# A hybrid decoder trunk on one core: the last half norm on two columns, wider output strips, and other DMA constants in the list scheduler

## The chip, the cores and the metric

The kernel runs on one NeuronCore of one Trainium2 chip. The metric is the device time in microseconds (us) of one execution. Three runs of the kernel before took 1483.68, 1481.92 and 1483.88 us; their median is 1483.68 us. With three runs spread over 2 us, differences of about 0.2% (3 us) can be told from none.

## What is computed

Two decoder layers over 512 tokens of width 1024, all in float32. Layer 0 mixes tokens with multi-scale retention, layer 1 with an mLSTM; each is followed by a convolutional feed-forward block. Every block is entered through an RMS norm with shift, scale and gate from a conditioning vector, and a last RMS norm ends the trunk:

```python
for i in range(2):
    h = rmsnorm(x, norm_tok_g[i]) * (1 + sc_t) + sh_t
    x = x + gt_t * (retention_mixer(h) if i == 0 else mlstm_mixer(h))
    h = rmsnorm(x, norm_ffn_g[i]) * (1 + sc_f) + sh_f
    x = x + gt_f * conv_ffn(h)
return rmsnorm(x, final_g)     # x * rsqrt(mean(x*x, -1) + 1e-6) * final_g
```

## The kernel before, in words

**Layout.** The residual stream lies transposed in SBUF: eight tiles `x[0]` to `x[7]` of 128 channels by 512 tokens (KT = 8). Every float32 product is made of three products of rounded parts (`mm3`, L654): a high part (`hi`, written by a copy on ACT into float32r) and a low part (`lo`, the rest). The low part of a weight comes either from one subtraction on DVE (`low_part`, L500) or from a negated copy on ACT followed by a DMA that accumulates the raw weight onto it, issued by GpSimd (`low_part_added`, L505). Weights are loaded by plain DMAs on SyncE's queue (SP), 512 KB each. Many projections are done with a seven-product block scheme (`Fold`, L547), whose sums of weight blocks are made on DVE (tiles `ws`, `wt`).

**Buffers.** Weights and all that is made from them share 18 wide slots (tag `w`: `raw`, `wa`, `wb`, `whi`, `wlo`, `ws`, `wt`, `wv`, `out`), and activations share 62 slots (tag `s`). Two more slots (tag `a`) serve the loads of the conditioning weights (`ada`) and of the down projection inside the feed-forward loop (`Beside`, L527).

**Who sets the order.** The program is first recorded as a list of calls, then a list scheduler orders it (`Plan`, L149), and each engine executes its calls in that order. For each call it has a modelled duration. `order` (L218) gives each call a due time: TensorE's calls follow one another without gaps, and every other call is due early enough for the calls that need it, less its own duration and a tail. `tail` (L261) is a short latency for engine work; for a plain DMA it is its transfer time plus 3.0 us, for an accumulating one plus 4.5 us. `run` (L264) then simulates the engines. A plain DMA of 512 KB takes 0.4 us of SP's time, then waits until 1.2 us have gone by and the modelled DMA is free, moves for 1.33 us, and counts as landed 1.2 us later (L357; 2.4 us for an accumulating one). Among the ready calls of an engine, the one with the earliest due time goes first. A call that opens a new buffer may start only if its buffer ranks, by due time, within the free slots of its kind (`makers`, L293), and not over 35 us ahead of its due time (EARLY). The scheduler's times exist only to choose an order; on the chip, semaphores hold each call until its data is there.

**The feed-forward loop.** `Ffn.items` (L1435) runs units 4 to 21 of the 22 pairs of up-projection tiles as 18 repeated units of one seven-product scheme each, in both layers (`folded`, L867), with the down projection of earlier groups inside (`downs`, L1439).

**The end.** The last group of the down projection is done in two halves of 256 tokens (`boundary`, L1067; HALVES, L59): eight `po` products for the first half, then eight for the second. After each product DVE adds it to `x[m]` (`add_residual`, L1031), ACT squares the half (`SquareSum.add`, L679) and DVE adds the squares up. In the second half the last two tiles' squares are not added but multiplied in directly (`direct = (0, 2)`, L1217). The root of the mean of squares (`SquareSum.root`, L694) is a product with a 128 by 128 matrix of 1/1024, so all 128 partitions hold the mean of each of the 256 tokens; then ACT takes a square root and DVE a reciprocal, both over 128 by 256 elements. `End.use` (L1222) multiplies each tile by its gain and the root in one DVE instruction and sends the output: the first half in two DMAs of four tiles while the second half is computed, the second half at the very end in four DMAs of two tiles (`End.rest`, L1240).

The same norm is already done on columns at the start of the program (`means`, L1602, and L1656 to L1666): there the tokens lie on partitions, four columns of 128, and are turned back by a product with a unit matrix. Its rows in the trace serve the prediction.

Of the kernel before, what the change touches and what calls it, by code (L numbers as in the profile page):

```python
# [10 lines left out]
F32 = mybir.dt.float32  # L11
F32R = mybir.dt.float32r
I32 = mybir.dt.int32
AF = mybir.ActivationFunctionType
ALU = mybir.AluOpType

P = 128
T = 512
D = 1024
KT = D // P  # L20
# [6 lines left out]
GROUPS = [4, 4, 4, 4, 6]  # L27
# [5 lines left out]
VADDED = (1, 6, 5, 7, 3)  # L33
SWAPPED = (64, 67, 75, 150, 153, 158, 188, 192, 200, 208, 209, 211, 222, 241, 287, 301, 313)
FOLD_FROM = 4
WPAD = 64
OFF = 16
DIRECT = (0, 0)
# [21 lines left out]
HA, HB = slice(0, 256), slice(256, 512)  # L60
# [88 lines left out]
class Plan:  # L149
# [109 lines left out]
        return self.run()  # L259

    def tail(self, c):  # L261
        return c.lat if not c.dma else c.dma + (4.5 if "accum_op" in c.k else 3.0)

    def run(self):  # L264
        calls = self.calls
# [3 lines left out]
        pe_at, lag, dma_free, table, issued = 0, 0.0, 0.0, None, set()  # L269
# [55 lines left out]
        while len(out) < len(calls):  # L325
            if not any(best.values()):
                held = [(calls[n].eng, calls[n].name, [b.args[4] for b in calls[n].bufs])
                        for e in engines for _, n in wait[e][:4]]
                live = [(b.args[4], b.uses) for b in {id(b): b for c in calls for b in c.bufs}.values()
                        if b.bufs and b.log is None and b.uses]  # L330
                print(len(live), live)
                raise RuntimeError(f"{len(out)} of {len(calls)}: {[b.args[4] for b in calls[pe[pe_at]].bufs]} {held}")
            t, e, n = min(c for c in best.values() if c)
            c, dirty = calls[n], {e}
            for b in c.bufs:
                if b.log is not None:
                    b.log, b.busy = None, 0.0
                    if b.bufs:
                        b.at = room[b.key].pop(0)[1]
                        dirty.update(engines)  # L340
                        makers[b.key].remove(b.maker)
            occ = c.occ
            if e == "POOL" and c.shared:
                port = (t, t + occ)
            elif e == "DVE" and c.shared:
                occ += SHARE * max(0.0, min(t + occ, port[1]) - max(t, port[0]))
            if c.fn and c.fn != table:
                table, occ = c.fn, occ + 1.3
            wait[e].remove((c.due, n))
            if e == "PE":  # L350
                issued.add(n)
                while pe_at < len(pe) and pe[pe_at] in issued:
                    pe_at, lag = pe_at + 1, t - calls[pe[pe_at]].due
            free[e] = t + occ
            if c.dma:
                dma_free = max(dma_free, t + occ + 1.2) + c.dma
                c.end = dma_free + (2.4 if "accum_op" in c.k else 1.2)  # L357
            else:
                c.end = t + occ + c.lat
            for b in c.bufs:  # L360
                b.busy = max(b.busy, c.end)
                b.uses -= 1
                if not b.uses and b.bufs:
                    insort(room[b.key], (b.busy, b.at))
                    dirty.update(engines)
            for m, real in c.succs:
                s = calls[m]
                s.left -= 1
                s.ready = max(s.ready, c.end if real else t + occ)
                if not s.left:  # L370
                    dirty.add(s.eng)
                    insort(wait[s.eng], (s.due, m))
            out.append(n)
            self.log.append((t, n, occ))
            for d in dirty:
                best[d] = choose(d)
# [10 lines left out]
def trunk(ctx: ExitStack, tc: tile.TileContext, xT, cb, pos, vec, ident, decay, zmask, ada, w_s0, w_in0, w_v0,  # L387
# [13 lines left out]
    def uid(s):  # L401
        count[0] += 1
        return f"{s}_{count[0]}"

    def tile_of(pool, shape, dt, tag, name):
        return Buf(pool, shape, dt, tag, name, KINDS.get(tag, 0), tag == "ps")

    def slot(s, dt=F32, w=T):
        return tile_of(slots, [P, w], dt, "s", uid(s))

    def wide(s, dt=F32):
        return tile_of(wpool, [P, WCOLS + WPAD], dt, "w", uid(s))

    def bank(s):
        return tile_of(psum, [P, T], F32, "ps", uid(s))
# [4 lines left out]
    def fixed(pool, shape, dt, name):  # L420
        b = tile_of(pool, shape, dt, name, name)
        b.get()
        return b

    plan = Plan()
    V, A, G, PE, S = (plan.engine(*p) for p in (("DVE", nc.vector), ("ACT", nc.scalar), ("POOL", nc.gpsimd),
                                                ("PE", nc.tensor), ("SP", nc.sync)))
# [4 lines left out]
    ones = {}  # L432
    for name, v in (("d", 1.0 / D), ("v", 1.0 / DV), ("1", 1.0)):
        o = fixed(const, [P, P], F32R, f"ones_{name}")
# [8 lines left out]
    x = [slot("x") for _ in range(KT)]  # L443
# [11 lines left out]
    def col(name, i):  # L455
        return vecs[:, VEC[name] + i : VEC[name] + i + 1]

    eps_t = fixed(const, [P, 1], F32, "eps_t")
# [53 lines left out]
    class Chunk:  # L512
        def __init__(self, src, n, off, added=False):
            self.off, self.added = off, added
            self.raw = wide("raw")[:, off : off + n]
            S.dma_start(self.raw, src)
# [151 lines left out]
    def reciprocal_root(dst, src, r, bias):  # L668
        A.activation(dst[:, r], src, AF.Sqrt, bias=bias)
        V.reciprocal(dst[:, r], dst[:, r])  # L670

    class SquareSum:

        def __init__(self, r, direct):
            self.r, self.acc, self.last, self.direct = r, slot("ssq"), [], direct

        def add(self, m):  # L679
            r = self.r  # L680
            if m == 0:
                A.activation(self.acc[:, r], x[0][:, r], AF.Square)
                return
            sq = slot("sq")
            A.activation(sq[:, r], x[m][:, r], AF.Square)
            if m >= KT - self.direct:
                self.last.append(sq)
            else:
                V.tensor_tensor(self.acc[:, r], self.acc[:, r], sq[:, r], op=ALU.add)
            if m == KT - self.direct - 1:  # L690
                self.parts = Pair("ss")
                self.parts.split(self.acc[:, r], r)

# [29 lines left out]


    items, steps_at = [], []
    now = ["start"]

# [27 lines left out]
    def item(uses, fn, free=True):  # L755
        for u in uses:
            if u.first is None:
                u.first = len(items)
            u.last = len(items)
        items.append((uses, fn, free))  # L760
        steps_at.append(now[0])
# [317 lines left out]
        norm.rest()  # L1079

    class Norm:
        direct = DIRECT

        def __init__(self):
            self.s, self.rs, self.xg = [None, None], [None, None], [{}, {}]
# [2 lines left out]
        def square(self, p, m):  # L1088
            r = slice(*HALVES[p])
            if m == 0:  # L1090
                self.s[p] = SquareSum(r, self.direct[p])
            self.s[p].add(m)
            if m in POOLED:
                self.xg[p][m] = slot("xg")
                A.activation(self.xg[p][m][:, r], x[m][:, r], AF.Copy, scale=self.gain(m))
# [118 lines left out]
    class End(Norm):  # L1214


        direct = (0, 2)  # L1217

        def gain(self, m):
            return col("final", m)  # L1220

        def use(self, p, k0, k1):  # L1222
            r = slice(*HALVES[p])
# [14 lines left out]
                self.use(0, 2 * k - 4, 2 * k)  # L1238

        def rest(self):  # L1240
            item([], lambda w: self.root(1))
            for k in range(0, KT, 2):
                item([], lambda w, k=k: self.use(1, k, k + 2))

    def scores(q, k, hd, weigh, total=None):

# [112 lines left out]
    class Ffn:  # L1359
# [75 lines left out]
        def items(self, norm):  # L1435
            w = w_up[self.layer]
            folds = [Fold((w[f], w[f + FT])) for f in range(FOLD_FROM, FT)]
            pairs = [self.steps(f) for f in range(FOLD_FROM, FT)]
            downs = [None] * (5 - FOLD_FROM) + [p for gi in range(len(GROUPS) - 1) for p in self.down(gi)]  # L1439
            steps, run = folded(folds, self.h, self.start.sums.terms, pairs, downs,  # L1440
                                dict(SIDES).get(f"fold{self.layer}", 0))
            now[0] = f"up{self.layer}"

            def early(n):
                todo = [steps.pop(0) for _ in range(n)]
                item([], lambda w: [f() for f in todo])
            self.up(2)
            early(1)
            th = self.pair(3)
            proj_item(w[3], self.h, th, True)  # L1450
            early(len(steps))
            proj_item(w[3 + FT], self.h, lambda ps: (self.start.sums.turn(), th(ps)), True)
            now[0] = "fold"
            item([], run)
            now[0] = f"end{self.layer}"
            boundary([], self.down(len(GROUPS) - 1), norm)
# [436 lines left out]
    for n, (uses, fn, free) in enumerate(items):  # L1893
# [11 lines left out]
        at = same.index(n)  # L1905
# [117 lines left out]
```

## Time and profile before

The profiled execution took 1483.41 us; its span from the first to the last instruction is 1481.6 us.

| | |
|---|---|
| median of three runs | 1483.68 us |
| profiled execution, its own time | 1483.41 us |
| its span | 1481.6 us |
| TensorE busy | 1461.3 us, 99% of the span |
| VectorE (DVE) busy | 1268.1 us, 86% |
| ScalarE (ACT) busy | 1075.9 us, 73% |
| DMA | 315.65 MB, mean 213 GB/s |
| mean granted TensorE clock | 0.997 |

PE is TensorE. An engine's row in a view gives a start or a busy time in microseconds, the engine, the operation, the written tile and the tiles read (`out<-in`), shapes, and in square brackets the idle time just before it with what ended that. All calls are issued from one line (L383), so tiles tell them apart. Matmuls overlap in TensorE's pipeline: the mean duration of one is longer than the distance between two, and a float32 matmul (not float32r) shows as two records.

### The profile page before, as it was taken

The numbers are of one execution on the slowest core, as the hardware profiler recorded it, in microseconds if no ns is written. First come the engines' busy times: TensorE is split into PE (matmuls) and PEld (weight loads), VectorE is DVE, ScalarE is ACT, GpSimd is POOL, SyncE is SP. The second block draws the span as 40 slices with busy tenths as digits, with TensorE's granted clock in tenths as the row PEclk, the third lists the DMA queues.
The fourth block names the chain that finished last, engine by engine and source line by source line (L and its number), as shares of the span: only waits on it lengthen the run. The fifth ranks groups of instructions, "written<-read, shape, count | busy, mean of one in ns | idle before, by whom it ended". The sixth has DMA issues, their size and how long they took to land.

```text
span 1481.6 us, 27248 instructions
## 1 busy us (share of the span) xinstructions
PE 1461.3 (99%) x10468; PEld 1368.8 (92%) x10468; DVE 1268.1 (86%) x2136; ACT 1075.9 (73%) x1606; POOL 279.0 (19%) x313
## 2 busy tenths in 40 slices
PE   9999999999999999999999999999999999999997
PEld 6799999998999999999999998999889899999997
DVE  7999979777989889898897999999889887777786
ACT  5678768777577676676668986989856876767662
POOL 0334132322111111111001222132211111111100
PEclk9999999999999999999999999999999999999998
DMA  9868989888798899999457895888687887888751
GB/s 363 252 175 207 282 209 230 224 250 212 206 215 215 241 261 258 265 261 266 118 180 171 207 246 144 208 221 199 205 239 201 213 219 194 194 208 191 190 125 58
DMA packets 93268, 315.65 MB, mean 213 GB/s; under 512 B 12225, under 2 KB 14657, under 8 KB 93138
## 3 DMA queue, kind: packets, MB, share of 16 engines
q0 software_dynamic: 32112, 116.54, 42.2%
q1 hardware_dynamic: 60738, 197.11, 38.3%
q8 instruction: 82, 1.34, 0.4%
q10 hardware_dynamic: 288, 0.27, 0.1%
q14 instruction: 48, 0.39, 0.1%
HBM read 195.23 MB, written 2.12 MB: 133 GB/s over the span
## 4 chain that ended last, share of the span: by engine, by line
PE 86%; DMA 7%; DVE 3%; ACT 2%; issue 2%; POOL 0%; DVEq 0%; ACTq 0%; SPq 0%; POOLq 0%
PE p L383 36%; PE po L383 27%; PE pv L383 9%; PE pav L383 4%; PE pp L383 3%; PE pf L383 3%; DMA wlo<-raw 2%; PE psc L383 2%; DMA raw<-w_in 1%; DMA wb<-w_up 1%; DMA raw<-w_dn 1%; PE pst L383 1%; DMA wlo<-wa 1%; DMA raw<-w_up 1%; PE pms L383 1%
## 5 line engine op out<-in xcount | busy, mean ns | idle before, releaser
L383 PE MATMUL p<-hh,whi 128*128 128x256 f32 (+1 forms) x994 | 275.6, 278 | 1.9 <-DVE p L383 1.9
L383 PE MATMUL p<-hl,whi 128*128 128x256 f32 x992 | 275.1, 277 | 0.0
L383 PE MATMUL p<-hh,wlo 128*128 128x256 f32 x992 | 273.4, 277 | 0.0
L383 ACT ACTIVATE wlo<-whi 128x1024 fp32r<-128x1024 f32 x223 | 235.0, 1057 | 39.8 <-PE po L383 15.1
L383 PEld LDWEIGHTS p<-hh,whi 128*128 128x128 f32 x994 | 187.1, 188 | 2.8 <-DVE p L383 2.3
L383 PEld LDWEIGHTS p<-hl,whi 128*128 128x128 f32 x992 | 186.7, 188 | 0.4
L383 PEld LDWEIGHTS p<-hh,wlo 128*128 128x128 f32 x992 | 185.6, 188 | 0.0
L383 PE MATMUL p<-t24h,whi 128*128 128x256 f32 x744 | 165.0, 279 | 4.1 <-ACT fs L383 3.1
L383 PE MATMUL po<-ggl,whi 128*128 128x512 f32 (+1 forms) x448 | 153.3, 343 | 0.0
L383 PE MATMUL po<-ggh,wlo 128*128 128x512 f32 (+1 forms) x448 | 153.1, 343 | 0.0
L383 PE MATMUL po<-ggh,whi 128*128 128x512 f32 (+1 forms) x448 | 152.4, 343 | 0.0
L383 ACT CAST whi<-raw 128x1024 fp32r<-128x1024 f32 (+1 forms) x117 | 118.0, 1019 | 44.8 <-DMA raw<-w_s 10.5
L383 PE MATMUL p<-t24l,whi 128*128 128x256 f32 x496 | 137.5, 277 | 0.0
L383 DVE SCALAR_TENSOR_TENSOR x<-po,mod,x 128x512 f32<-128x512 f32 (+1 forms) x184 | 113.0, 628 | 23.2 <-PE po L383 22.7
L383 PEld LDWEIGHTS p<-t24h,whi 128*128 128x128 f32 x744 | 126.3, 188 | 6.9 <-ACT fs L383 3.9
L383 DVE SCALAR_TENSOR_TENSOR ada<-ada,c_ext 128x1025 f32<-128x1025 f32 x96 | 119.5, 1246 | 6.5 <-DMA ada<-ada 6.4
L383 POOL DMA_DIRECT2D wlo<-wa x62 | 53.8, 867 | 355.4 <-ACT wlo L383 223.4
L383 PE MATMUL po<-yh,whi 128*128 128x256 f32 (+1 forms) x354 | 116.0, 329 | 0.3 <-ACT o L383 0.3
L383 PE MATMUL po<-yl,whi 128*128 128x256 f32 (+1 forms) x352 | 115.7, 329 | 0.0
L383 PE MATMUL po<-yh,wlo 128*128 128x256 f32 (+1 forms) x352 | 115.6, 329 | 0.0
L383 DVE SCALAR_TENSOR_TENSOR cv<-p,vecs,cv 128x511 f32<-128x511 f32 (+1 forms) x144 | 106.4, 744 | 9.9 <-ACT cv L383 9.2
L383 ACT CAST whi<-ws 128x1024 fp32r<-128x1024 f32 x86 | 90.0, 1050 | 28.5 <-DVE ws L383 23.5
(287 smaller groups left out, 4422.0 us busy)
## 6 DMA issues: line engine op xcount, KB each, us to landing
ada<-ada SPq DMA_DIRECT2D x96, 512.5 KB, 7.4
wlo<-ws POOLq DMA_DIRECT2D x68, 512.0 KB, 6.9
wlo<-wa POOLq DMA_DIRECT2D x62, 512.0 KB, 6.3
wlo<-wt POOLq DMA_DIRECT2D x44, 512.0 KB, 6.9
wlo<-raw POOLq DMA_DIRECT2D x41, 512.0 KB, 8.4
wa<-w_up SPq DMA_DIRECT2D x36, 512.0 KB, 6.9
wb<-w_up SPq DMA_DIRECT2D x36, 512.0 KB, 6.2
raw<-w_o SPq DMA_DIRECT2D x32, 512.0 KB, 6.6
```

What stands on the lines that cost most here:

```text
L383: getattr(c.obj, c.name)(*[real(v) for v in c.a], **{key: real(v) for key, v in c.k.items()})
```

## The change

The change has three parts.

- The scheduler lets a plain DMA land 2.0 us after its modelled transfer instead of 1.2 (`LANDING`), and wants it 4.0 us plus transfer ahead of its use instead of 3.0 (`LEAD`). The constants for accumulating DMAs stay. No call is added or removed by this; the order that the scheduler finds may differ anywhere in the program.
- The second half of the last norm: the added squares and the last two tiles' squares are each multiplied with one column (float32, two matmuls of 128 tokens each), which gives the means in two columns; ACT and DVE take root and reciprocal over 128 by 2 elements; two products with the unit matrix (loaded once more, 64 KB) spread them over the partitions in PSUM. The split of the added squares into two parts goes (`bare`).
- The second half's outputs: ACT multiplies each tile by its gain as soon as it is there (eight `Copy` instructions with a scale); DVE multiplies three tiles, three tiles, one tile and one tile by the root, and each of the four is one DMA.

`LATER` replaces a written 5; the list of `None` before `downs` has one entry before and after.

```diff
+LATER = 5
+LANDING = (2.0, 2.4)
+LEAD = (4.0, 4.5)
...
     def tail(self, c):
-        return c.lat if not c.dma else c.dma + (4.5 if "accum_op" in c.k else 3.0)
+        return c.lat if not c.dma else c.dma + LEAD["accum_op" in c.k]
...
-                c.end = dma_free + (2.4 if "accum_op" in c.k else 1.2)
+                c.end = dma_free + LANDING["accum_op" in c.k]
...
-            if m == KT - self.direct - 1:
+            if m == KT - self.direct - 1 and not self.bare:
...
     class End(Norm):
-        direct = (0, 2)
+        direct, bare = (0, 2), True
+        strips = ((0, 3), (3, 6), (6, 7), (7, 8))
...
+        def square(self, p, m):
+            super().square(p, m)
+            if p:
+                for k0, k1 in self.strips:
+                    if k0 <= m < k1:
+                        if m == k0:
+                            self.scaled[k0] = wide("xg")
+                        at = (m - k0) * 256
+                        A.activation(self.scaled[k0][:, at : at + 256], x[m][:, HB], AF.Copy, scale=self.gain(m))
+
+        def last_root(self):
+            if self.eye is None:
+                self.eye = slot("eye")
+                S.dma_start(self.eye[:, :P], ident)
+            s, ps, out_ps, rc = self.s[1], bank("pms"), bank("pst"), slot("rc")
+            for n, sq in enumerate([s.acc] + s.last):
+                for t in range(2):
+                    PE.matmul(ps[:, t : t + 1], sq[:, 256 + t * P : 384 + t * P], ones["d"][:, :1].bitcast(F32),
+                              start=n + t == 0, stop=True, skip_group_check=True)
+            reciprocal_root(rc, ps[:, :2], slice(0, 2), eps_t[:])
+            for t in range(2):
+                PE.matmul(out_ps[:, 256 + t * P : 384 + t * P], rc[:, t : t + 1].broadcast_to([P, P]),
+                          self.eye[:, :P], start=t == 0, stop=True, skip_group_check=True)
+            self.rs[1] = out_ps
+
+        def last_use(self, k0, k1):
+            n = k1 - k0
+            o, each = wide("out"), lambda t: t.rearrange("p (a t) -> p a t", a=n)
+            V.tensor_tensor(each(o[:, : n * 256]), each(self.scaled[k0][:, : n * 256]),
+                            self.rs[1][:, HB].rearrange("p (a t) -> p a t", a=1).broadcast_to([P, n, 256]), op=ALU.mult)
+            S.dma_start(out[k0:k1, :, HB].rearrange("m p t -> p m t"), each(o[:, : n * 256]))
...
         def rest(self):
-            item([], lambda w: self.root(1))
-            for k in range(0, KT, 2):
-                item([], lambda w, k=k: self.use(1, k, k + 2))
+            item([], lambda w: self.last_root())
+            for k0, k1 in self.strips:
+                item([], lambda w, k0=k0, k1=k1: self.last_use(k0, k1))
...
-            downs = [None] * (5 - FOLD_FROM) + [p for gi in range(len(GROUPS) - 1) for p in self.down(gi)]
+            downs = [None] * (LATER - FOLD_FROM) + [p for gi in range(len(GROUPS) - 1) for p in self.down(gi)]
```

More of the change, by code (lines that the diff above doesn't have):

```diff
@@ L672, in trunk, with __init__ @@
     class SquareSum:
-        def __init__(self, r, direct):
-            self.r, self.acc, self.last, self.direct = r, slot("ssq"), [], direct
+        def __init__(self, r, direct, bare=False):
+            self.r, self.acc, self.last, self.direct, self.bare = r, slot("ssq"), [], direct, bare
         def add(self, m):
@@ L1081, in trunk @@
     class Norm:
-        direct = DIRECT
+        direct, bare, eye = DIRECT, False, None
         def __init__(self):
@@ L1090, in square @@
             if m == 0:
-                self.s[p] = SquareSum(r, self.direct[p])
+                self.s[p] = SquareSum(r, self.direct[p], self.bare and p)
             self.s[p].add(m)
@@ L1214, in trunk, with __init__ @@
     class End(Norm):
-        direct = (0, 2)
+        direct, bare = (0, 2), True
+        strips = ((0, 3), (3, 6), (6, 7), (7, 8))
+        def __init__(self):
+            super().__init__()
+            self.scaled = {}
         def gain(self, m):
             return col("final", m)
+        def square(self, p, m):
[27 more added lines that the diff above has]
+            S.dma_start(out[k0:k1, :, HB].rearrange("m p t -> p m t"), each(o[:, : n * 256]))
         def use(self, p, k0, k1):
```

## The prediction

> **What bounds the kernel now.** I read the page first, then who TensorE waited for, then the chain of waits over the last 12 us.
>
> ```profile
> PE 1461.3 (99%) x10468; PEld 1368.8 (92%) x10468; DVE 1268.1 (86%) x2136; ACT 1075.9 (73%) x1606; POOL 279.0 (19%) x313
> ```
>
> TensorE is busy for 1461.3 of 1481.6 us, so 20.3 us is all that order or a shorter tail can win; the change takes no product out of the body. The next rows say where these 20 us lie: the waits of PE from 100 to 1470 us, then the PE instructions that stood still longest (in brackets the idle time before them).
>
> ```profile
> PE p L383 <- ACT fs L383: 3.1, 4, 1.3
> PE p L383 <- DVE p L383: 2.9, 4, 1.3
> PE po L383 <- ACT o L383: 0.3, 1, 0.3
> ```
> ```profile
> 54.99 0.50 PE L383 MATMUL pst<-whi,hh 128*128 128x512 f32 x1 [0.95 <-ACT hh L383]
> 688.91 0.38 PE L383 MATMUL p<-t24h,whi 128*128 128x256 f32 x1 [1.26 <-ACT fs L383]
> 802.14 0.39 PE L383 MATMUL p<-t24h,whi 128*128 128x256 f32 x1 [0.66 <-DVE p L383]
> 1205.16 0.38 PE L383 MATMUL p<-t24h,whi 128*128 128x256 f32 x1 [0.30 <-ACT fs L383]
> 1214.00 0.39 PE L383 MATMUL p<-t24h,whi 128*128 128x256 f32 x1 [0.31 <-DVE p L383]
> ```
>
> The body loses 6.3 us (3.1 + 2.9 + 0.3) after 100 us and 0.95 us at 55 us: 7.3 us together. The rest lies in the start-up and in the end. The chain of waits through those five stalls:
>
> ```profile
> 41.25 11.95 DMA raw<-w_in
> 675.53 9.80 DMA raw<-w_dn
> 793.15 5.98 DMA wb<-w_in
> 1190.73 11.57 DMA wb<-w_up
> ```
>
> Each of the five ends a chain that starts with a plain load; these stalls add up to 0.95 + 1.26 + 0.66 + 0.30 + 0.31 = 3.5 us. The other 3.8 us of the 7.3 end in chains of engines or in accumulating DMAs. The end, in order of time:
>
> ```profile
> 1470.78 0.50 DVE x L383
> 1471.30 0.42 ACT sq L383
> 1471.77 0.71 PE pms L383 x2
> 1472.51 0.48 ACT rs L383
> 1473.01 1.76 DVE rs L383
> 1474.80 0.48 DVE out L383
> 1475.68 2.38 DVE out L383 x6
> ```
>
> SP's output DMAs at the end, and their median time from issue to landing:
>
> ```profile
> 1475.71 2.75 SPq L383 DMA_DIRECT2D out<-out  x4
> ```
> ```profile
> out<-out SPq DMA_DIRECT2D x4, 256.0 KB, 2.2
> ```
>
> Nothing overlaps here: from DVE's start at 1470.78, set free by the last product, each step waits for the one before, up to the first output DMA at 1475.71. From there to 1481.6 stand the remaining products, the transfers and the closing.
>
> **The tail, step by step.** Residual and square stay. For the rest, the rows of the start-up do the same on columns:
>
> ```profile
> 13.10 3.57 PE L383 MATMUL pms<-ones_d,sq 128*128 128x1 f32 x16 [1.44 <-DVE sq L383]
> 16.54 0.77 PE L383 MATMUL pst<-warm,ones 128*128 128x512 f32 x1
> 17.31 2.08 PE L383 MATMUL pms<-eye,rc 128*128 128x128 f32 x8
> 16.78 0.27 ACT L383 ACTIVATE rc<-pms,eps_t 128x4 f32<-128x4 f32 x1 [0.85 <-PE pms L383]
> 17.08 0.18 DVE L383 RECIPROCAL rc<-rc 128x4 f32<-128x4 f32 x1 [2.03 <-ACT rc L383]
> ```
> ```profile
> L383 PE MATMUL po<-ggl,whi 128*128 128x512 f32 x256 | 100.3, 392 | 0.0
> ```
> ```profile
> 1472.50:1474.00 1.50, 0.00 (x0) 0.00 (x0) 0.99 (x1) 0.47 (x1) 0.00 (x0) 1.00 0.00 0
> 1474.00:1474.50 0.50, 0.00 (x0) 0.00 (x0) 0.50 (x1) 0.00 (x0) 0.00 (x0) 0.50 0.00 0
> ```
>
> A float32 matmul shows as two records (two tiles of four columns are 8 matmuls, x16). At 13 us they ran at half rate: the 128x512 product took 0.77 us there and 0.392 later. So four records for the last tile's column take 4 x 3.57/16 = 0.89 us at half rate and about 0.5 at full rate, against 0.71 now; the columns of the other squares (eight records) run during residual and square, 1470.78 to 1471.72, where now PE works on the mean as well. The square root takes 0.27 for 0.48, the reciprocal 0.18 for 1.76. New is the product with the unit matrix: 4 x 2.08/8 = 1.04 us at half rate, 0.6 at full rate with its handoff. The two rows of windows (granted clock third from the right) show full clock until 1474.0, 1.5 us after PE's last product (1471.77 + 0.71 = 1472.48); the new products start near 1472.9, so I take full rate. Sum: -0.2 - 0.2 - 1.6 + 0.65 = -1.35 us. With both products at half rate it is 0.85 us less: -0.5, the other end.
>
> The Trainium skill, "TensorE: Matmul & The Clock Gate", section "What's actually happening", lets the clock fall to half after an idle window of about 3.4 us that runs free of the kernel. By that rule a window that fell a little earlier would give -0.5 and not -1.35; the trace agrees that the fall comes, but later than the place in question.
>
> The reciprocal is gone from the bound then, and the outputs are late next:
>
> ```profile
> L383 DVE TENSOR_TENSOR wlo<-raw,whi 128x768 fp32r<-128x768 f32 x45 | 42.9, 953 | 7.8 <-ACT whi L383 7.3 <-issue 0.3
> L383 DVE TENSOR_TENSOR z<-z,pmu 128x512 f32<-128x512 f32 x16 | 10.1, 679 | 0.2 <-PE pmu L383 0.2
> 1476.50:1479.80 3.30, 0.00 (x0) 0.00 (x0) 1.56 (x4) 0.00 (x0) 0.00 (x0) 0.50 0.90 318
> ```
>
> The first DMA waits for one product of 128x768 (0.95 us; an operand in PSUM, as in `pmu`, costs nothing extra: 0.679 for 512 columns) where it waited 0.91 (1474.80 to 1475.71): +0.05. All four products take about 0.87 + 0.87 + 0.33 + 0.33 = 2.4 us instead of 0.48 + 0.40 + 2.38 = 3.3. But 1.05 MB at 318 GB/s needs 3.3 us, and the window shows it moving from 1476.5 on without a break, so the end shifts with the first issue and not with the last product: -1.3. If the rate rises because DVE feeds it faster, only the last product counts: 1474.80 - 1.35 + 2.4 + 2.2 to landing = 1478.05 and 0.2 for two issues close together (an estimate), against 1475.68 + 2.38 + 2.2 = 1480.3 now: -2.0. **Tail: -1.3 us, from -0.5 to -2.0.**
>
> ```profile
> L383 ACT ACTIVATE sq<-x 128x256 f32<-128x256 f32 x14 | 5.8, 418 | 14.9 <-DVE x L383 14.9
> ```
>
> The eight scaled copies cost about 0.42 us each on ACT, which stands idle for 14.9 us before 14 squares in that stretch, over 1 us each: free. Only the last can be seen; it fits into PE's 0.5 us between square and root, and if it were put ahead of the square it would cost 0.4. The removed split (ACT and DVE, under 0.5 us each) lay ahead of the last product and gives nothing. The unit matrix, 64 KB, is loaded on SP beside the end's products, where SP has two DMAs to issue: nothing.
>
> **The scheduler's constants** have no row of their own: they add nothing and move instructions. I bound them.
>
> ```profile
> wa<-w_up SPq DMA_DIRECT2D x36, 512.0 KB, 6.9
> wv<-w_v SPq DMA_DIRECT2D x12, 512.0 KB, 3.7
> ```
> ```profile
> DVE ws L383 <- DMA wb<-w_up: 10.2, 5, 3.9
> ```
> ```profile
> SPq L383 <- PE p L383: 289.2, 74, 13.1
> ```
>
> In the model a lone 512 KB load lands 0.4 + 1.2 + 1.33 + 1.2 = 4.1 us after its issue, and 4.9 with the change; on the chip the median is 6.9 for the 36 loads of `wa` in the feed-forward, and 3.7 for the 12 of `wv`. So where the DMAs are busy, DVE and ACT have sums and casts in their queues too early, and what is queued behind them waits along: the sums `ws` held DVE up five times, once for 3.9 us, just ahead of the two stalls after 1202. A later landing puts other ready work in front; a due time 1 us earlier ranks a load's buffer before those of casts and sums due in that microsecond. Best case: all five stalls behind plain loads go, -3.5. Worst case: not below new stalls of the same kind elsewhere, +3.5, without the repeated case below. 0.8 + 1.0 us per load is two thirds of what `wa` comes late (6.9 - 4.1 = 2.8), and not every stall hangs on one load alone, so I take half of 3.5 back: **-1.7 us**.
>
> Sum: -1.3 - 1.7 = -3.0 us of the profiled execution's 1483.41 (0.3 below the median of the runs): **1480.4 us**.
>
> **The rivals.** *Only the tail.* SP issues plain transfers alone, and all of them are moved by the same 1.0 us, so their order among themselves stays; the row of SP's waits (74 waits, 289.2 us) says that a load starts when a product frees its slot, whatever its due time. Then the stalls stay, or as many come as go: -1.3, 1482.1 us; with the worst case of +3.5 it is 1485.6. A second way there: the old landing was long enough, as it is for `wv` (3.7 against 4.1), so a longer one lets no call pass that should have. Against both: ranks do change, and `wa` at 6.9 is far over 4.1.
>
> The Trainium skill, "DMA: Bandwidth & Descriptors", section "Anatomy of one DMA — SWDGE (gpsimd) path", speaks for that second way: it fits 2.0 us plus bytes over 436 GB/s per DMA, on GpSimd's path, which is 3.2 us for 512 KB and would leave 1482.1. The trace agrees with it near `wv` alone.
>
> *The tail at half rate.* A clock that falls before the new products leaves -0.5 of the tail: 1481.2 with the -1.7. Against it stand the two rows of the clock.
>
> *More than the loads.* A new order also clears stalls of engine chains. With all of the 3.5 and none to half of the other 3.8 it is -4.8 to -6.7, in the middle -5.7: 1477.7 us. For it: these waits too rest on the order in a queue. Against it: the constants concern plain loads alone. *Slower: the feed-forward unit.*
>
> ```profile
> 490.00:660.00 170.00, 170.00 (x1225) 158.83 (x1225) 150.41 (x259) 118.09 (x164) 25.04 (x29) 1.00 0.96 261
> ```
>
> There PE has no idle time at all over 170 us, with DMA 0.96 busy. If loads that rank earlier take slots from `whi` and `wlo`, a low part comes late in every one of the 36 units (18 in each layer). At 0.2 us each that is +7.2, less the tail's 1.3: 1489 us. It decides from 0.04 us a unit (1.3/36). Against it: no wait of PE shows there now, so some cover exists.
>
> **How the numbers follow.** Forecast (the tail, and a quarter to three quarters of the 3.5: 1479.5 to 1481.2) 0.36; the tail at half rate 0.06; only the tail 0.18; more 0.25; slower 0.15. About 0.2% (3 us) is what the measurement can tell. The forecast's middle lies on that line: 0.23 of it faster, 0.13 within. Faster 0.23 + 0.25 = 0.48; same 0.13 + 0.06 + 0.18 + 0.01 = 0.38; slower 0.14. The range runs from 1476.5, just under the -6.7 of the third case, to 1485.5, the tail with the worst case of new stalls; about 0.06 is left out below (the tail at its -2.0 end beside it) and 0.14 above.
>
> **What would show it.** In the changed profile: DVE's reciprocal at the end 0.18 us; the first output DMA 4.93 - 1.3 = 3.6 us after the last residual's start; the products with the unit matrix at full clock; PE's waits on `fs` and `p` from 100 to 1470 us at 6.0 - 2.5/2 = 4.7 us. Wrong if the rate of the outputs rises over 350 GB/s, if a PE wait appears inside 490 to 660 us, or if waits behind plain loads are as long as now.

## The result and the profile after

The changed kernel takes 1491.17 us (median of six runs), the kernel before 1483.07 us in the same comparison: ratio 1.0056, 95% interval 1.0045 to 1.0067, so it is slower by 0.6%. One of its six runs was slow, 1813.69 us at a granted clock of 0.75, and the ratio leaves it out. The forecast was 1480.4 us. The profiled execution took 1490.21 us, its span is 1488.4 us. First the row of busy times from the page of the changed kernel.

```profile
PE 1467.1 (99%) x10478; PEld 1373.6 (92%) x10478; DVE 1257.3 (84%) x2131; ACT 1079.6 (73%) x1612; POOL 279.8 (19%) x313
```

TensorE idles 1488.4 - 1467.1 = 21.3 us against 20.3 before. That looks like almost nothing, because the shorter end hides part of the idle time and a half-rate clock counts as busy. So the stretches must be read one by one. Windows of the changed kernel (start:end, length, then PE, PEld, DVE, ACT and POOL busy; the granted clock stands third from the right, the GB/s last):

```profile
53.00:57.00 4.00, 4.00 (x19) 3.34 (x18) 2.15 (x3) 2.62 (x3) 0.31 (x1) 1.00 1.03 368
100.00:1470.00 1370.00, 1359.39 (x9961) 1284.02 (x9960) 1160.20 (x1946) 1011.02 (x1506) 257.11 (x290) 1.00 0.81 209
490.00:660.00 170.00, 169.99 (x1224) 158.40 (x1224) 149.89 (x257) 119.16 (x165) 24.98 (x29) 1.00 0.95 254
655.00:700.00 45.00, 45.00 (x324) 41.91 (x323) 39.64 (x67) 30.50 (x44) 5.78 (x7) 1.00 0.99 279
798.00:806.00 8.00, 8.00 (x70) 8.00 (x69) 4.68 (x9) 4.81 (x9) 1.41 (x2) 1.00 1.00 199
800.00:1200.00 400.00, 392.02 (x2891) 372.01 (x2891) 355.67 (x594) 318.09 (x485) 89.56 (x100) 1.00 0.79 204
1195.00:1235.00 40.00, 40.00 (x292) 37.47 (x292) 32.93 (x55) 28.29 (x39) 6.02 (x7) 1.00 0.88 224
1484.00:1486.00 2.00, 0.00 (x0) 0.00 (x0) 0.55 (x2) 0.00 (x0) 0.00 (x0) 0.51 1.08 383
```

Two of the same windows before:

```profile
100.00:1470.00 1370.00, 1363.67 (x10025) 1290.17 (x10024) 1174.28 (x1961) 1009.90 (x1508) 254.50 (x288) 1.00 0.81 210
800.00:1200.00 400.00, 397.19 (x2943) 377.80 (x2942) 362.79 (x602) 323.89 (x494) 90.36 (x101) 1.00 0.82 209
```

The body idles 1370 - 1359.39 = 10.6 us now and 6.3 before. Where the five stalls behind plain loads stood (around 55, 690, 802 and from 1205 to 1214 us), PE has no gap left in this execution; whether the new order removed them is another question (see e7_low174). New ones came from 800 to 1200 us, mainly the second layer's mixer: 8.0 us of idle time there for 2.8. What PE waited for from 100 to 1470 us in the changed kernel (in total, times, longest):

```profile
PE p L386 <- DMA wlo<-wa: 4.1, 2, 2.8
PE p L386 <- ACT fs L386: 2.2, 3, 1.5
PE psc L386 <- ACT mqkh L386: 1.8, 1, 1.8
PE p L386 <- DVE p L386: 1.5, 3, 0.9
```

The old causes fell from 3.1 and 2.9 to 2.2 and 1.5 us; new are waits for an accumulating DMA (4.1) and for a cast on ACT ahead of a product of the mLSTM (1.8). The same work in both chains of waits dates the loss. The changed kernel:

```profile
772.43 21.53 PE pv L386 x95
903.87 21.77 PE po L386 x96
1163.77 21.78 PE pp L386 x96
```

and the kernel before:

```profile
771.36 21.77 PE pv L383 x96
897.16 21.77 PE po L383 x96
1154.31 21.78 PE pp L383 x96
```

At the ends of these rows (start plus length) the lag is 0.8, 6.7 and 9.5 us, and 1479.17 - 1470.78 = 8.4 us at the last residual. A lag of 1.0 us is there at 67 us already (the first long row of `pp` starts at 67.18 for 66.21), and it is no work of the order: the first products of this execution ran slow for longer. The same four products in both kernels, the changed one first:

```profile
24.15 1.91 PE L386 MATMUL pst<-wlo,hh 128*128 128x512 f32 x4
22.45 1.07 PE L383 MATMUL pst<-wlo,hh 128*128 128x512 f32 x4
```

When this slow start ends differs between executions that have the same order there: at about 20 us before, and at about 24 us in e1_tail below, which has the order of before up to the end and yet is one of the two fastest kernels; its granted clock reads 0.50 from 14.2 to 24.3 us. Here it ends at about 26 us. So a lag of 1 us between two single executions need not come from the order; the medians of the runs decide.

The rest comes in lumps, and the largest stands at 821 us. PE's row there (with the idle time before it), the DMA in the chain of waits, the windows in the wait and behind it, and four of PE's products, two in the second window and two behind it:

```profile
824.05 0.38 PE L386 MATMUL p<-hh,wlo 128*128 128x256 f32 x1 [2.76 <-DMA wlo<-wa]
```
```profile
814.38 9.63 DMA wlo<-wa
```
```profile
821.10:824.00 2.90, 0.19 (x2) 0.00 (x0) 2.62 (x5) 2.90 (x7) 0.86 (x1) 1.00 1.09 260
825.30:828.60 3.30, 3.30 (x18) 3.30 (x17) 0.33 (x2) 1.11 (x2) 0.00 (x0) 0.50 1.06 279
```
```profile
827.46 0.41 PE L386 MATMUL p<-hl,whi 128*128 128x256 f32 x1
827.67 0.41 PE L386 MATMUL p<-hh,wlo 128*128 128x256 f32 x1
828.84 0.28 PE L386 MATMUL p<-hh,wlo 128*128 128x256 f32 x1
828.95 0.28 PE L386 MATMUL p<-hh,whi 128*128 128x256 f32 x1
```

The accumulating DMA of a low part was issued at 814.38 and took 9.63 us. Before, the DMA for this low part was issued at 811.37; now ACT has a table load of 1.28 us and an activation of 0.63 us ahead of the negated copy to which the DMA adds. PE stood for 2.76 us, and the clock of the stretch after it was half for some 3.4 us: products of one shape start 0.21 us apart there and 0.11 us apart behind it, which loses some 1.6 us. Wait and half clock are 2.76 + 1.6 = 4.4 us, of which the idle time shows only the first. The lag agrees: it is 0.8 us at 794 us and 5.1 us at the next long row of `pv` (849.97 for 844.84).

The end did what it should. The chain of waits of the changed kernel, and SP's output DMAs:

```profile
1479.17 0.49 DVE x L386
1479.69 0.42 ACT sq L386
1480.16 0.62 PE pms L386 x4
1480.80 0.27 ACT rc L386
1481.09 0.18 DVE rc L386
1481.32 0.72 PE pst L386 x4
1482.06 0.95 DVE out L386
```
```profile
1483.05 2.31 SPq L386 DMA_DIRECT2D out<-out  x4
```

From the last residual to the end of the span it is 1488.4 - 1479.17 = 9.2 us, against 1481.6 - 1470.78 = 10.8 before: 1.6 us less. So some 10 us were lost ahead of the end, and the end gave 1.6 back.

### The profile page after: what moved, and what is told of

It reads as the page before. It is cut to its first block, busy times and chain, and to the rows that moved or that the text cites. A ratio compares the mean times of both kernels' runs of the same rounds, so it can differ in the third digit from the quotient of the medians.

```text
span 1488.4 us, 27225 instructions
## 1 busy us (share of the span) xinstructions
PE 1467.1 (99%) x10478; PEld 1373.6 (92%) x10478; DVE 1257.3 (84%) x2131; ACT 1079.6 (73%) x1612; POOL 279.8 (19%) x313
## 4 chain that ended last, share of the span: by engine, by line
PE 88%; DMA 5%; issue 2%; ACT 2%; DVE 2%; POOL 1%; DVEq 0%; ACTq 0%; POOLq 0%
PE p L386 36%; PE po L386 28%; PE pv L386 7%; PE pav L386 4%; PE pp L386 3%; PE pf L386 3%; PE pst L386 2%; PE psc L386 2%; DMA wlo<-ws 1%; DMA wlo<-wa 1%; DMA wlo<-raw 1%; PE pc L386 1%; DMA wlo<-wv 1%; PE pms L386 1%; ACT whi L386 0%
```

## The experiments

All kernels compute everything. All but the kernel before have the new end, and the edits are against the changed kernel. Intervals are 95%.

**The end alone.** The first theory: the end gives what its steps say and the order of the body costs the rest. The rival: the new end itself costs something.

```diff
-LANDING = (2.0, 2.4)
-LEAD = (4.0, 4.5)
+LANDING = (1.2, 2.4)
+LEAD = (3.0, 4.5)
```

> The new end with the old constants (1.2 and 3.0). On every engine the order up to the last feed-forward unit is that of before, so only the end differs. My theory (the constants cost the time, the end saves some): from the last residual's start to the end of the span 9.2 us as in the changed kernel, against 10.8 before, so 1.6 us under before, ratio 0.9989. Rival (the end's eight copies, the fourth load and the products in float32 cost more than they save): at or over before, ratio 1.000 to 1.003.

Measured: 0.9988 (0.9980 to 0.9997), 1480.94 us for 1482.59. The rival falls. In its chain the residual starts at 1470.10 in a span of 1479.4, an end of 9.3 us, as in the changed kernel. So the constants cost 1.0056/0.9988 = 1.0068, about 10 us, and e1_tail is the kernel to compare the rest with.

**Each constant alone**, on the new end: only `LANDING = (2.0, 2.4)`, and only `LEAD = (4.0, 4.5)`.

> The new end, a landing of 2.0 us, but the old lead of 3.0. If the later landing in the simulated run makes the order that costs the time (a load that counts as late lets other calls go ahead on ACT, and the low parts behind them come late): 6 to 9 us over the new end alone, with waits of TensorE for accumulating DMAs in the mLSTM's projections. If the earlier due time of loads does it (buffers ranked ahead of casts and sums): within 2 us of the new end alone.

> The new end, the lead of 4.0 us, but the old landing of 1.2. The mirror of the run before: if the rank of buffers costs the time, 6 to 9 us over the new end alone; if the later landing does it, within 2 us of it. If any reordering of this program costs about the same (third theory), both runs are 5 to 10 us over it.

Measured: 1.0047 (1.0034 to 1.0060) and 1.0024 (1.0014 to 1.0035); over e1_tail 0.59% and 0.36%. Neither of the two is the culprit by itself. Both cost, as the third theory in the expectation of e3_lead has it.

**The same constants in one part of the program.** A call takes the new constants only where it was recorded in a step of the feed-forward blocks or of the end (e4_ffn_only), or only outside these (e5_mixers_only, with `not in` in the last line):

```diff
+LATE = ("up0", "up1", "fold", "end0", "end1")
+LANDING = (1.2, 2.4), (2.0, 2.4)
+LEAD = (3.0, 4.5), (4.0, 4.5)
...
+        return c.lat if not c.dma else c.dma + LEAD[c.late]["accum_op" in c.k]
...
+                c.end = dma_free + LANDING[c.late]["accum_op" in c.k]
...
+        plan.late = int(steps_at[n] in LATE)
```

> The new end; the new constants only for calls recorded in the feed-forward steps, the old ones for both mixers. In the changed kernel the feed-forward steps won 0.7 us near 452, 1.5 at 687 and 1.5 at 1205, and the mixers lost the rest. If the constants are good where loads are the wait and bad where accumulating DMAs are: 5 us under before (1.6 from the end, 3.7 from the feed-forward), 1478. If any reordering costs, stalls come at other places and it is at or over 1483.

> The mirror of e4: the new end, the new constants only outside the feed-forward steps, the old ones inside them. If the loss sits in the order of the mixers, it is all here, and the 2 to 3 us that the feed-forward won are missing: 1.005 to 1.008. If the loss came from the feed-forward or from the crossings between them, 0.999 to 1.002.

Measured: e4_ffn_only 0.9985 (0.9976 to 0.9993), 1479.91 us, which can't be told from e1_tail, so the 3.7 us expected from the feed-forward didn't come; e5_mixers_only 1.0006 (0.9996 to 1.0016), 1482.82 us. The theory that the mixers carry the loss falls with that: by themselves they cost 0.18% over e1_tail, hardly more than the intervals, the feed-forward steps nothing, and both together 0.68%. The parts don't add up, so the loss has no place of its own.

**One stall taken away.** The low part that PE waited for at 821 us is the 174th in the program. One number more in the list `SWAPPED` (L34), which names the low parts made the other way than their group, has DVE subtract it:

```diff
-SWAPPED = (64, 67, 75, 150, 153, 158, 188, ...
+SWAPPED = (64, 67, 75, 150, 153, 158, 174, 188, ...
```

> The changed kernel with one low part, the first weight of the mLSTM's second q and k scheme, made by a subtraction on DVE instead of a copy on ACT and an accumulating DMA. TensorE waited 2.8 us for that DMA at 821 us, and its clock fell to half for 3.4 us just behind (825 to 829). If that wait is what the stage lost, the 5 us between 812 and 837 us come back and the run is 3 to 5 us under the changed kernel, ratio to before 1.002 to 1.004. If other waits stand close behind it, it gains under 2 us.

Measured: 1.0030 (1.0018 to 1.0042), 1487.51 us, which is 0.26% or 3.9 us under the changed kernel. PE's row at that place and the two windows, in this kernel:

```profile
822.17 0.39 PE L386 MATMUL p<-t24h,whi 128*128 128x256 f32 x1 [0.93 <-DVE p L386]
```
```profile
821.10:824.00 2.90, 1.97 (x17) 1.83 (x16) 2.90 (x7) 2.90 (x7) 0.00 (x0) 1.00 1.08 333
825.30:828.60 3.30, 3.30 (x21) 3.05 (x20) 3.30 (x7) 3.27 (x6) 0.86 (x1) 1.00 0.72 217
```

The wait of 2.76 is gone, a smaller one of 0.93 us stands in its place, and the clock stays full. Up to 800 us every engine has its instructions in the changed kernel's order here, as the lists of the two programs show, so the place can be compared directly: the long row of `pv` behind it starts at 846.66 for 849.97 us, with 772.38 and 772.43 at the row ahead. That is 3.3 us. Behind the place the order differs again (at some 600 of ACT's 1600 places), so the 3.9 us of the medians are this stall and a new order of the rest in one. Still 0.42% over e1_tail is left, in other places.

The equal order up to 800 us shows something else. In this execution the start ran fast (the long row of `pp` starts at 66.24 us, as before), and two of the stalls behind plain loads that the changed kernel's profile had lost stand again:

```profile
55.06 1.20 PE L386 MATMUL pst<-whi,hh 128*128 128x512 f32 x4 [1.00 <-ACT hh L386]
689.81 0.39 PE L386 MATMUL p<-t24h,whi 128*128 128x256 f32 x1 [1.35 <-ACT fs L386]
```

So the new order by itself had not removed these two. That they were missing in the changed kernel's profile belongs to that execution; its later start is the likely reason, which no run shows.

**The other direction, and constants that have nothing to do with landing.** e6_back lets plain loads land earlier than the old constants do (`LANDING` 0.8, `LEAD` 2.5). e8_nudge keeps the old constants and makes the modelled transfer of a load 1% longer; e9_actlat keeps them and adds 0.01 us to ACT's modelled latency. If the old constants are better because they describe the DMAs better, the nudges should cost nothing; if the order as such was fitted, any other order costs.

```diff
-            c.dma = size * (5.4 if "accum_op" in k else 2.45) + 0.05
+            c.dma = size * (5.4 if "accum_op" in k else 2.47) + 0.05
...
-    LAT = dict(PE=0.23, DVE=0.18, ACT=0.18, POOL=0.2, SP=0.1)
+    LAT = dict(PE=0.23, DVE=0.18, ACT=0.19, POOL=0.2, SP=0.1)
```

> The new end; landing 0.8 us instead of 1.2 and lead 2.5 instead of 3.0, the opposite direction. If later loads as such cost the time, this is as fast as the new end alone or faster: ratio to before 0.998 to 0.999. If any other order of this program costs (the old constants' order is a good one among many), it is 3 to 8 us over the new end alone: 1.001 to 1.005.

> The new end and the old landing and lead; in the scheduler's model alone a plain DMA moves 2.47 us per MB instead of 2.45 (0.01 us for a load of 512 KB). No engineer would mean anything by that, but some 700 of 1600 positions on ACT change. If the cost of the change is the cost of any other order, 2 to 6 us over the new end alone, ratio 1.000 to 1.003. If it is the 0.8 and 1.0 us themselves, equal to the new end alone: 0.998 to 0.9995.

> As the nudge, but with no DMA in it: the model's latency behind an ACT call is 0.19 us instead of 0.18. Same two answers: 1.000 to 1.003 if any other order costs, 0.998 to 0.9995 if only later loads do.

Measured: e6_back 1.0103 (1.0085 to 1.0122), 1497.86 us; e8_nudge 1.0032 (1.0019 to 1.0045), 1487.62 us; e9_actlat 1.0032 (1.0023 to 1.0042), 1488.00 us. Two nudges of no meaning cost 0.44% over e1_tail each, and the other direction costs more than either answer expected. What PE waited for most in e8_nudge, and two of its rows:

```profile
PE p L386 <- ACT fs L386: 5.6, 3, 3.0
PE p L386 <- DVE p L386: 1.8, 3, 0.8
PE pav L386 <- ACT sh L386: 1.7, 1, 1.7
PE p L386 <- DMA wlo<-ws: 1.4, 1, 1.4
PE p L386 <- DMA wlo<-wt: 1.2, 1, 1.2
```
```profile
319.65 0.39 PE L386 MATMUL p<-t24h,whi 128*128 128x256 f32 x1 [3.04 <-ACT fs L386]
542.38 0.39 PE L386 MATMUL p<-t24h,whi 128*128 128x256 f32 x1 [2.08 <-ACT fs L386]
```

Its stalls are as large as those of the changed kernel and stand at other places behind other engines. How far the lists of instructions move says why: by tile names, without buffer numbers, another operation than in e1_tail stands at some 560 of ACT's 1600 places and some 800 of DVE's 2035 in e8_nudge, and at nearly 1000 of each in the changed kernel.

**More draws.** e14_old_243 has 2.43 in place of 2.45 and e17_old_dvelat DVE's latency at 0.19, both with the old constants; e10_noswap_old has them with an empty `SWAPPED`. The same nudges with the new constants: e12_new_nudge (2.47), e15_new_243 (2.43), e16_new_actlat (ACT 0.19), e11_noswap_new (empty list). e13_back_nudge is e6_back with 2.47, e18_ffn_nudge has old constants everywhere and 2.47 in the feed-forward steps alone.

```diff
-SWAPPED = (64, 67, 75, 150, 153, 158, 188, 192, 200, 208, 209, 211, 222, 241, 287, 301, 313)
+SWAPPED = ()
```

> The new end, the old constants, and an empty list SWAPPED: the 17 low parts that the list moves between DVE and the accumulating DMAs go back. If the old order was good because this list was fitted to it, the run loses what a nudge loses, 5 to 8 us over the new end alone (ratio to before 1.002 to 1.005). If the list does not matter, 0.998 to 0.9995.

> The changed kernel with the list SWAPPED empty. If the changed constants lose only because the list fits the old order, then without the list they are level with the old constants without it (the run before this one, within 0.15%). If the later landing and the lead are worse in themselves, this one is slower than that one by 0.3 to 0.6%.

> The changed kernel with the nudge of 2.47 us per MB. If each order is a draw and the changed one an ordinary draw, this is another: 1.001 to 1.007, and it may fall on either side of the changed kernel's 1.0056. If the constants themselves cost 0.68%, 1.005 to 1.0065.

> Landing 0.8 and lead 2.5 with the same nudge. Without the nudge they gave 1.0103. If earlier modelled landings are worse in themselves, again over 1.007; if that was a bad draw, 1.001 to 1.006.

> The new end and the old constants, nudged the other way: 2.43 us per MB. A third draw with the old constants (two gave 1.0032 and 1.0032). If the constants themselves matter, again about 1.003 and the two new draws of this call at 1.0055 to 1.0065; if only the draw matters, anything from 0.999 to 1.007 on both sides.

> The changed kernel nudged to 2.43 us per MB, the partner of the run before. Constants matter: 1.0055 to 1.0065, 0.25% or more over its partner. Only the draw: no fixed sign against its partner.

> The changed kernel with the ACT latency of 0.19 us, the partner of the old constants with it (1.0032). Constants matter: 1.0055 to 1.0065. Only the draw: anything from 0.999 to 1.007.

> The new end, the old constants, and a model latency behind DVE of 0.19 us instead of 0.18: a fourth draw with the old constants. Constants matter: about 1.003. Only the draw: anything from 0.999 to 1.007. If the old order itself is a lucky draw, it is over 0.9988 in any case.

> The new end, the old constants, and the nudge of 2.47 us per MB only for loads recorded in the feed-forward steps; the second layer's mixer then keeps its order on ACT and DVE. If a nudge costs through the mixers alone, 0.998 to 0.9995 as the new end alone; if any other order anywhere costs, 1.001 or more.

Measured, ratio to the kernel before with its interval:

| | old constants | new constants |
|---|---|---|
| as written | e1_tail 0.9988 (0.9980 to 0.9997) | changed kernel 1.0056 (1.0045 to 1.0067) |
| 2.47 | e8_nudge 1.0032 (1.0019 to 1.0045) | e12_new_nudge 1.0065 (1.0051 to 1.0079) |
| 2.43 | e14_old_243 1.0047 (1.0035 to 1.0059) | e15_new_243 1.0120 (1.0107 to 1.0133) |
| ACT 0.19 | e9_actlat 1.0032 (1.0023 to 1.0042) | e16_new_actlat 1.0058 (1.0046 to 1.0070) |
| DVE 0.19 | e17_old_dvelat 1.0060 (1.0048 to 1.0072) | not run |
| empty list | e10_noswap_old 1.0053 (1.0041 to 1.0066) | e11_noswap_new 1.0065 (1.0053 to 1.0078) |

Besides these, e18_ffn_nudge 1.0016 (1.0007 to 1.0025) and e13_back_nudge 1.0138 (1.0121 to 1.0156). e12_new_nudge lies where both of its answers meet, and e15_new_243 lies above both of its own, so neither decides between them. Three readings follow.

- Four nudges of the old constants give 1.0032 to 1.0060, 0.44 to 0.72% over e1_tail. The old order is a lucky one or a fitted one, and leaving it can cost about what the change cost (0.68%). Not every other order costs as much: e18_ffn_nudge moves some 250 of ACT's places for 0.28%, and e4_ffn_only some 540 for nothing that can be told.
- With an empty list the old constants give 1.0053 and the new ones 1.0065. The 17 entries of `SWAPPED` are worth 0.65% (1.0053/0.9988) in the old order and 0.09% in the new, an amount within the intervals. So the list suits this one order.
- At the same nudge or list the new constants are worse in four of four pairs, by 0.33, 0.73, 0.26 and 0.12%, the last within the intervals. That may be a small cost of the constants themselves or the luck of four draws. Earlier landing was bad in both draws (1.0103, 1.0138).

The body's idle time follows the ratios. Windows from 100 to 1470 us of e1_tail, e10_noswap_old and e15_new_243, in this order:

```profile
100.00:1470.00 1370.00, 1364.54 (x10035) 1291.28 (x10034) 1175.38 (x1961) 1013.04 (x1515) 254.62 (x290) 1.00 0.81 210
```
```profile
100.00:1470.00 1370.00, 1359.23 (x9956) 1283.86 (x9955) 1160.01 (x1941) 1013.04 (x1509) 261.19 (x291) 1.00 0.82 211
```
```profile
100.00:1470.00 1370.00, 1352.55 (x9858) 1275.69 (x9857) 1157.81 (x1936) 1004.13 (x1495) 259.11 (x290) 1.00 0.81 209
```

PE idles 5.5, 10.8 and 17.4 us there, with no, one and three half-rate stretches of 3.4 us. The DMA rate is the same within 1%: the transfers have not become slower on the whole, the work comes at other moments.

## Why the prediction was wrong

**The tail (-1.3 us) was right.** The medians of e1_tail give -1.7 us, the traces -1.6. To the first output product it takes 1482.06 - 1479.17 = 2.89 us for 4.02 (1474.80 - 1470.78): -1.13 where -1.35 was worked out, because the four records of the column took 0.62 us, not 0.5, and the unit matrix 0.72, not 0.6. The reciprocal took 0.18 as predicted and the first output DMA started 3.88 us after the residual, not 3.6. The new products ran at full clock: it fell only around 1484. One step was wrong and in favour: 318 GB/s was taken as the limit of the outputs, and with three tiles to each of the first two DMAs they moved at 383 (the text had named 350 as the mark of this mistake). Why they moved faster no run separates. From the first output DMA to the end of the span it is 1488.4 - 1483.05 = 5.35 us for 5.89, and that made up for the slower products, so the size of the tail is right in part by luck.

**The scheduler's constants (-1.7 us) were the step that failed.** The gain that the forecast named is not shown. In the profile the five stalls behind plain loads are gone, and the waits on `fs` and `p` fell to 3.7 us, below the 4.7 that was the test. But in e7_low174, with the same order up to 800 us, the two at 55 and 689 us stand, so the order alone did not bring that pass. And the sum counted only what could come back, and bounded the harm by "not below new stalls of the same kind elsewhere, +3.5". The new stalls are not of the same kind. The largest stand behind an accumulating DMA, whose constants were not touched, and behind a cast for a product of the mLSTM, and in place of -1.7 us the constants cost 10. The reason that led there: the prediction read the five stalls as the model's faults, to be cured by a truer constant, while e8_nudge, e9_actlat, e14_old_243 and e17_old_dvelat show that the order before is better than these neighbours: each of the four changes of a constant lost, whatever it meant. The term that was missing is the price of a new order; these four put it at 0.44 to 0.72%, e18_ffn_nudge at 0.28% and e4_ffn_only at nothing.

**The rivals.** *Only the tail* is what e1_tail runs, and it came to 1480.94 us; but with the constants in place it wasn't what happened, and its premise that SP's transfers keep their order fell: another transfer than before stands at some 80 of SP's 410 places. *More than the loads* is refuted by the sign. *Slower through the feed-forward unit* had the sign and nearly the time (1489) with the wrong place: from 490 to 660 us PE is busy for 169.99 of 170 us. No unit of the loop pays there; the loss that the trace shows comes in a few stalls of 1 to 3 us, one of them with a half-rate clock behind it. The half rate after a stall lay outside the prediction's price for one.

**What stays open.** Whether the new constants cost anything of their own beside the lost order (four of four pairs say so, by 0.12 to 0.73%), and why the two halves of the program cost 0.18% and nothing by themselves and 0.68% together. Of the 10 us, one stall is shown by a run (3.3 us at its place, e7_low174); the others are read from the trace alone. How many of the five old stalls the new constants remove is open too. Of all these kernels e1_tail and e4_ffn_only are the fastest, and they can't be told apart.

## What to carry to other kernels

When a kernel's order comes out of a list scheduler and hand-made lists were fitted on top of it, a change of a model constant is a new draw of the order: price it by nudging a constant that means nothing, more than once, since the draws here cost from 0 to 0.7%, and not by the stalls that it should remove. Don't read a stall as gone from one execution. Test the parts of a mixed change one at a time, since here a sure gain of 1.6 us was buried under 10. Read a stall of TensorE of over 2 us with the windows behind it: the half clock that followed cost more than half as much again.

## What the runs showed of the hardware

- *The clock falls late and after short waits.* After the wait of 2.76 us that ended at 824.05 it was half from about 825.3 to 828.7, when PE was busy again. In e8_nudge two waits show the same, ended at 319.65 (3.04 us) and at 542.38 (2.08 us):

```profile
321.10:324.30 3.20, 3.20 (x17) 3.20 (x17) 1.12 (x2) 2.79 (x5) 0.00 (x0) 0.50 1.05 396
542.90:546.20 3.30, 3.30 (x14) 3.01 (x14) 3.30 (x8) 0.77 (x2) 0.86 (x1) 0.50 0.76 194
```

  Waits of 1.26 us (before, at 688.91) and of 1.33 and 1.76 us (the changed kernel, ended at 883.12 and 959.40) had no such stretch, while one of 1.75 us in e15_new_243, ended at 967.40, had one:

```profile
969.10:972.40 3.30, 3.30 (x18) 3.30 (x17) 1.32 (x3) 1.34 (x3) 0.86 (x1) 0.50 1.08 243
```

  So the length of the wait alone doesn't decide it. The Trainium skill, "TensorE: Matmul & The Clock Gate", section "What's actually happening", lets the clock fall after an idle window of about 3.4 us. The length of the half-rate stretches here, some 3.4 us, agrees with such a window; the idle time doesn't, since 1.75 us were enough once, and the fall came when work had been back for 0.5 to 1.7 us.
- *Transfers above 358 GB/s.* The end's transfers to HBM moved at 383 GB/s over 2 us. The plain loads of the start-up moved faster still, 416 GB/s over 20 us (before):

```profile
10.00:30.00 20.00, 17.87 (x71) 14.04 (x71) 17.45 (x31) 9.11 (x13) 0.00 (x0) 1.00 1.03 416
```

  The Trainium skill, "DMA: Bandwidth & Descriptors", section "Where 436 GB/s comes from", has about 358 GB/s bind transfers between HBM and SBUF: on this one core both the loads and the outputs were above it.
- *An accumulating DMA under load* took 9.63 us at the stall for 512 KB, where plain loads of that size in the feed-forward have medians of 6.3 (`wa`) and 8.0 (`wb`), and the accumulating ones of `wa` 6.9 (all in the changed kernel).
